# Summing the squares of two token blocks on TensorE, k-tile by k-tile, instead of on VectorE

## The chip, the cores and the metric

The kernel runs on one core of one Trainium2 chip. The metric is the device time of one execution in microseconds (us); the time before is the median of three runs. The engines are named as the profile names them: PE is TensorE (PEld its weight loads), DVE is VectorE, ACT is ScalarE, POOL is GpSimd, SP is SyncE, whose queue issues nearly all DMAs here.

## The reference, cut to what matters

One decoder layer over 2048 tokens and 1024 channels, float32. What the change touches is the first normalisation, of the layer's input x:

```
h = rmsnorm(x, g_mix) * (1.0 + sc_m) + sh_m     # x32 * rsqrt(mean(x32 * x32, over channels) + EPS) * g
proj = h @ w_in                                 # columns: q | k | v | forget gate | u
```

sc_m and sh_m come from the conditioning vector c: silu(c) @ w_ada + b_ada. After the projection come attention with a forget gate on q, k, v, a state-space scan on u (its tables are worked out in the kernel), an output projection, and a gated MLP.

## The kernel before, in words

The tokens are cut into four blocks of 512 (TB), the channels into eight k-tiles of 128 (KT). x lies transposed: a tile `xt` holds two k-tiles of one block, 128 channels on the partitions and 512 tokens along the free axis. So the sum of squares of a token runs over partitions and over k-tiles.

`load_x(b)` (L400) does this for a block. For each of the four `xt` tiles it issues a load on SP (L404), and for each of its two k-tiles ACT squares it: the first square goes straight into an accumulator `sq_acc` (L330), the seven others into a buffer `sq` of two (L333), which DVE adds to the accumulator (L334). `norm_factor` (L355) then sums over the partitions: `token_sums` (L339) takes each 128 tokens of the accumulator as weights and a column of ones as the moving operand, four matmuls into four columns of a PSUM bank `misc_ps` (L342; eight instructions in the trace). `rsqrt_mean` (L163) works out 1/sqrt on DVE in some twelve small operations on 128x4 numbers, `spread` (L362) transposes the result over all partitions on PE (L348) and ACT copies it to `rt` (L368).

`proj_u(b, ...)` (L432) uses it: `modulate` (L387) makes, for each k-tile, `h_f` = x * scale * rt on DVE (L392), stores it for blocks 2 and 3 (L395, SP), and splits it into a high half on ACT (`h_hi`, L380) and a low half on DVE (`h_lo`, L381). The projection's matmuls (L429) take three products per k-tile: high by high weight, high by low weight, low by high weight.

At the program's begin the blocks come in the order 2, 3, 1, 0. Before block 2 can be modulated, the scale and shift of the first normalisation have to be there: `ada_first` (L275) loads 32 tiles of w_ada and takes half of them through PE (L286) and half through DVE (L288, L290); each half of the channels ends with small matmuls of one moving column (L317, L299) and a small addition on DVE (`mod_gm`, `mod_sm`; L319, L294, L300). The tables of the state-space part (`ssm_tables`, L640 on, `tb_` tiles) are many small and some middling operations on DVE in the same stage, with small matmuls of their own on PE (L777, L778). Weight tiles are split into a high half on ACT and a low half on DVE as well (L77, L78).

No order is written out by hand for this stage. The code gives the operations in program order, and when the program is built, a planner lays out every engine's queue from a simulated timeline (`schedule_with_timeline_sim=True`, L1728); each engine then runs its queue in that fixed order and waits where an operand isn't ready. So an edit can change the order of instructions that it doesn't mention.

The lines of the stage:

```
rows0 = load_x(2)
wu = load_u_weights(wup, vfu_slots[4:6])
ada_first()
batches = ssm_tables(pp)
wu += load_u_weights(wup, vfu_slots[6:8])
...
for b in (2, 3, 1):
    h = proj_u(b, rows0 if b == 2 else load_x(b), wu)
```

Of the kernel before, what the change touches and what calls it, by code (L numbers as in the profile page):

```python
# [12 lines left out]
F32 = mybir.dt.float32  # L13
# [3 lines left out]
AF = mybir.ActivationFunctionType  # L17
# [5 lines left out]
P = 128  # L23
S = 2048
D = 1024
KT = D // P
NB = 4
TB = S // NB
# [11 lines left out]
XB = 6  # L40
# [3 lines left out]
HOOK = 5  # L44
EACH = 1
LEAD = 4
NSC = 2


# [62 lines left out]
def hybrid_layer(ctx, tc, x, c_t, w_ada, b_col, gains, w_flat, bf_row, a_re, a_im, log_dt,  # L112
                 sb_re, sb_im, sc_re, sc_im, dskip, glu, bglu, conv, out):
    nc = tc.nc
    V, A, G, T, Q = nc.vector, nc.scalar, nc.gpsimd, nc.tensor, nc.sync
# [20 lines left out]
    ones = const.tile([P, 1], F32, name="ones")  # L136
# [26 lines left out]
    def rsqrt_mean(ss, n, width):  # L163

        v = small.tile([P, 8], F32, name="rs_v")[:, :n]
        V.tensor_scalar(out=v, in0=ss, scalar1=1.0 / width, scalar2=EPS, op0=ALU.mult, op1=ALU.add)
        i = small.tile([P, 8], I32, name="rs_i")[:, :n]
        V.tensor_scalar(out=i, in0=v.bitcast(I32), scalar1=1, scalar2=None, op0=ALU.logical_shift_right)
        V.tensor_scalar(out=i, in0=i, scalar1=-1.0, scalar2=RSQRT_MAGIC, op0=ALU.mult, op1=ALU.add)
        y = i.bitcast(F32)  # L170
        for _ in range(3):
            t = small.tile([P, 8], F32, name="rs_t")[:, :n]
            r = small.tile([P, 8], F32, name="rs_y")[:, :n]
            V.tensor_tensor(out=t, in0=y, in1=y, op=ALU.mult)
            V.scalar_tensor_tensor(out=t, in0=t, scalar=-0.5, in1=v, op0=ALU.mult, op1=ALU.mult)
            V.scalar_tensor_tensor(out=r, in0=t, scalar=1.5, in1=y, op0=ALU.add, op1=ALU.mult)
            y = r
        return y
# [53 lines left out]
    xp = in_ctx.enter_context(tc.tile_pool(name="x", bufs=3))  # L232
# [5 lines left out]
    def misc_ps():  # L238
        return in_ps.tile([P, 512], F32, name="misc_ps", tag="misc", bufs=1)
# [85 lines left out]
    sq_pool = [xp]  # L325

    def sum_squares(acc, first, src, cols, eng, tmp=None):

        if first:
            A.activation(acc[:, cols], src, AF.Square)  # L330
        else:
            sq = sq_pool[-1].tile([P, TB], F32, name="sq", tag="sq", bufs=2)[:, cols] if tmp is None else tmp
            A.activation(sq, src, AF.Square)  # L333
            eng.tensor_tensor(out=acc[:, cols], in0=acc[:, cols], in1=sq, op=ALU.add)  # L334

    def sq_acc():
        return sq_pool[-1].tile([P, TB], F32, name="sq_acc", tag="sq_acc", bufs=2)

    def token_sums(ps, acc, s0, n):  # L339

        for i in range(n):
            T.matmul(ps[:, i : i + 1], lhsT=acc[:, (s0 + i) * P : (s0 + i + 1) * P], rhs=ones[:, 0:1],  # L342
                     start=True, stop=True)

    def over_channels(ps, r, n):

        for i in range(n):
            T.transpose(ps[:, i * P : (i + 1) * P], r[:, i : i + 1].broadcast_to([P, P]), ident)  # L348
# [6 lines left out]
    def norm_factor(acc, ps_fn, direct=False):  # L355

        ps = ps_fn()
        token_sums(ps, acc, 0, 4)
        r = rsqrt_mean(ps[:, 0:4], 4, D)
        return spread(r, ps_fn, direct)  # L360

    def spread(r, ps_fn, direct=False):  # L362
        ps = ps_fn()
        over_channels(ps, r, 4)
        if direct:
            return ps
        rt = sq_pool[-1].tile([P, TB], F32, name="rt", tag="rt", bufs=RT)
        A.copy(rt, ps)  # L368
        return rt
# [28 lines left out]


    def load_x(b):  # L400
        rows, acc = [], sq_acc()
        for j in range(4):
            xt = xp.tile([P, 2, TB], F32, name="xt", tag="xt", bufs=XB)
            Q.dma_start(xt, x[b, j])  # L404
            rows.append(xt)
            for a in range(2):
                sum_squares(acc, j == 0 and a == 0, xt[:, a], slice(0, TB), V)
        return rows, norm_factor(acc, misc_ps)

    def load_u_weights(pool, slots):  # L410
        res = []
        for so, sn, n in slots:
            hi = pool.tile([P, sn], F32R, name="wu_hi", tag="wu_hi", bufs=4)
            lo = pool.tile([P, sn], F32R, name="wu_lo", tag="wu_lo", bufs=4)
            weights.load(so, sn, hi, lo)
            res.append((hi, lo))
        return res
# [644 lines left out]
    def attention(blocks, lead=0):  # L1062

        heads = [(b, h) for b in blocks for h in range(H)]
        steps, cur = att_max(*heads[0])
        for f in steps:
            f()
        for j, (b, h) in enumerate(heads):
            nsteps, nxt = att_max(*heads[j + 1]) if j + 1 < len(heads) else ([], None)
            msteps, done = att_main(b, h, *cur), 0  # L1070
            for n, f in enumerate(msteps):
                f()
                todo = min(len(nsteps), -(-len(nsteps) * (n + 1) // max(1, len(msteps) - lead)))
                while done < todo:
                    nsteps[done]()
                    done += 1
            cur = nxt
# [31 lines left out]
    with tc.tile_pool(name="prep", bufs=1) as pp, tc.tile_pool(name="wu", bufs=1) as wup:  # L1109
# [5 lines that stand above are left out]
        marks = []  # L1115
        for b in (2, 3, 1):
            h = proj_u(b, rows0 if b == 2 else load_x(b), wu)
            marks.append(mark[0])
        batches(marks + marks[-1:])
        rows0 = load_x(0)  # L1120
        proj_qkv(1, h, pair_ps(qs_psum))
        ada_late(4, "gf")
        h = proj_u(0, rows0, wu)
        ada_late(3, "sf")
        forget()
        ada_cols()
        fold_gain(mod["gf"], 8)
        ada_late(2, "tm")
# [105 lines left out]
    def h2_of(b, xs, acc):  # L1234
        ps_fn = ff_ps if b == 0 else op_ps
        return modulate(xs, norm_factor(acc, ps_fn, True), mod["gf"], mod["sf"])
# [308 lines left out]
    with tc.high_priority():  # L1545
        x1, sq1 = out_proj(0, mt)
        yt += [y_tile(d, F32) for d in range(8)]
        h2 = h2_of(0, x1, sq1)
    attention((1, 2, 3), LEAD)
    att_ctx.close()  # L1550
# [17 lines left out]
    def block3():  # L1568

        steps = up_rows(ops["f1"], h_rows(xb, spread(ops["r3"], op_ps, True)))  # L1570
        rows = next(steps)
        for nm in ("b11", "b21"):
            ops[nm] = [split_h(f) for f in rows[nm]]
        next(steps)
        ops["t1"] = [split_h(f, parts=late_pair(late, 14)) for f in rows["t1"]]
        next(steps)
        spare = [f("hh", [P, TB + 2 * (f is vq_a)], F32R)[:, 0:TB] for f in (vq_b, vq_c, vq_a) for _ in range(2)]
        ops["t2"] = [split_h(f, parts=late_pair(late, 14) if k < 3 else spare[0:2]) for k, f in enumerate(rows["t2"])]
        next(steps)
        ops["b22"] = [split_h(rows["b22"][k], parts=spare[2 + 2 * k : 4 + 2 * k]) for k in range(2)]  # L1580
        return steps, rows

    for b in range(2):
        i = 0
        for g, n in enumerate(FFG):
# [7 lines left out]
            sq = sq_acc() if last else None  # L1593
            if last:
                mt = mix_t(b + 1)
            for d in range(8):
# [12 lines left out]
                if last and d == OPD + 1:  # L1609
                    with behind():  # L1610
                        if b == 0:
                            h2 = modulate(x1n, spread(r, op_ps, True), mod["gf"], mod["sf"])
                        else:
                            ops["r3"] = r
                            steps, rows = block3()
# [117 lines left out]
```

## Time and profile before

| | us |
|---|---|
| median of three runs | 2649.02 |
| the three runs | 2645.67, 2649.02, 2649.54 |
| the profiled execution | 2642.66 |
| its span, first to last instruction | 2641.0 |
| PE busy in the span | 2553.1 |
| DVE busy | 1925.0 |
| ACT busy | 1237.9 |

The mean granted clock of PE over the span is 0.984. A busy PE need not be PE at its peak: matmuls are pipelined, their ends are modelled, and in stages where the granted clock is below 1 the same matmul takes longer. In a timeline row stand the start, the duration, engine, line, operation, output and inputs, shape and count, and in brackets the idle time of the engine before it and what ended it. Where one row holds several instructions, its duration is that of the whole row. Instructions on DVE and ACT overlap a little, so the next one can start before the one before has ended.

### The profile page before, as it was taken

The numbers are of one execution on the slowest core, as the hardware profiler recorded it, in microseconds if no ns is written. First come the engines' busy times: TensorE is split into PE (matmuls) and PEld (weight loads), VectorE is DVE, ScalarE is ACT, GpSimd is POOL, SyncE is SP. The second block draws the span as 40 slices with busy tenths as digits, with TensorE's granted clock in tenths as the row PEclk, the third lists the DMA queues.
The fourth block names the chain that finished last, engine by engine and source line by source line (L and its number), as shares of the span: only waits on it lengthen the run. The fifth ranks groups of instructions, "written<-read, shape, count | busy, mean of one in ns | idle before, by whom it ended". The sixth has DMA issues, their size and how long they took to land. (4 is left out here: it accounts for less than half of the span.)

```text
span 2641.0 us, 35638 instructions
## 1 busy us (share of the span) xinstructions
PE 2553.1 (97%) x12343; PEld 2067.4 (78%) x12343; DVE 1925.0 (73%) x3568; ACT 1237.9 (47%) x2056; POOL 190.2 (7%) x146
## 2 busy tenths in 40 slices
PE   6999999999999999999999999999989999999997
PEld 3888877887788887888778887888758888887886
DVE  7989588966887877886877777675687777773343
ACT  3423255553564545564645555565544444442222
POOL 0001000000000000000000000000043333320000
PEclk8999999999999999999999999999989999999999
DMA  8486987667466565655657565547632332346563
GB/s 311 155 272 212 302 261 208 204 195 248 139 200 218 187 199 164 204 191 186 200 174 231 170 202 168 188 164 259 222 104 104 112 112 96 122 150 249 168 233 99
DMA packets 265925, 500.63 MB, mean 190 GB/s; under 512 B 27120, under 2 KB 111984, under 8 KB 265744
## 3 DMA queue, kind: packets, MB, share of 16 engines
q1 hardware_dynamic: 263920, 493.10, 56.7%
q0 software_dynamic: 1280, 4.20, 0.4%
q8 instruction: 98, 1.61, 0.2%
q10 hardware_dynamic: 544, 1.05, 0.1%
q14 instruction: 83, 0.68, 0.1%
HBM read 371.17 MB, written 127.01 MB: 189 GB/s over the span
## 5 line engine op out<-in xcount | busy, mean ns | idle before, releaser
L78 DVE TENSOR_TENSOR w_lo<-w_raw,w_hi 128x1024 fp32r<-128x1024 f32 (+2 forms) x219 | 235.8, 1078 | 206.9 <-ACT w_hi L77 205.0
L77 ACT CAST w_hi<-w_raw 128x1024 fp32r<-128x1024 f32 (+2 forms) x219 | 203.1, 929 | 354.2 <-DMA w_raw<-in_w_flat 110.1
L1248 PE MATMUL ff_ps<-h_lo,w_hi 128*128 128x512 f32 x704 | 279.9, 398 | 0.8 <-DVE h_lo L381 0.8
L1248 PE MATMUL ff_ps<-h_hi,w_lo 128*128 128x512 f32 x704 | 280.2, 398 | 0.0
L1248 PE MATMUL ff_ps<-h_hi,w_hi 128*128 128x512 f32 x704 | 279.4, 399 | 0.0
L999 DVE TENSOR_TENSOR pl<-pf,ph 128x512 fp32r<-128x512 f32 (+1 forms) x320 | 194.8, 618 | 19.6 <-ACT ph L998 18.4
L998 ACT CAST ph<-pf 128x512 fp32r<-128x512 f32 (+1 forms) x320 | 177.9, 569 | 60.9 <-PE o_ps L1008 54.8
L1007 DVE TENSOR_TENSOR acc<-acc,pf 128x512 f32<-128x512 f32 (+2 forms) x264 | 159.2, 604 | 28.2 <-ACT pf L997 25.7
L1248 PEld LDWEIGHTS ff_ps<-h_lo,w_hi 128*128 128x128 f32 x704 | 133.4, 190 | 29.5 <-DVE h_lo L381 1.1
L1248 PEld LDWEIGHTS ff_ps<-h_hi,w_lo 128*128 128x128 f32 x704 | 133.4, 189 | 29.3 <-DMA w_lo<-wlo 0.4
L997 ACT ACTIVATE pf<-sc_ps 128x512 f32<-128x512 f32 (+2 forms) x184 | 98.4, 539 | 123.1 <-PE sc_ps L988 73.0
L1248 PEld LDWEIGHTS ff_ps<-h_hi,w_hi 128*128 128x128 f32 x704 | 133.2, 189 | 28.8 <-issue 0.2
L107 ACT CAST w_hi<-w_raw 128x1024 fp32r<-128x1024 f32 (+2 forms) x100 | 96.4, 964 | 102.9 <-PE ff_ps L1222 41.1
L1281 PE MATMUL ff_ps<-act_lo,w_hi 128*128 128x512 f32 x352 | 139.5, 397 | 0.0
L1280 PE MATMUL ff_ps<-act_hi,w_hi 128*128 128x512 f32 x352 | 139.3, 398 | 0.2 <-ACT rt L368 0.2
L1282 PE MATMUL ff_ps<-act_hi,w_lo 128*128 128x512 f32 x352 | 139.3, 397 | 0.0
L949 DVE TENSOR_REDUCE mx<-sc_ps 128x1 f32<-128x512 f32 (+2 forms) x164 | 97.5, 599 | 49.1 <-PE sc_ps L944 24.6
L1008 PE MATMUL o_ps<-ph,vv 128*128 128x512 f32 (+1 forms) x320 | 120.5, 377 | 2.3 <-ACT ph L998 2.2
L1371 PE MATMUL up_x<-hh,w_hi 128*128 128x512 f32 x352 | 113.4, 401 | 7.6 <-DVE hh L378 5.9
L1012 PE MATMUL o_ps<-pl,vv 128*128 128x512 f32 (+2 forms) x312 | 115.9, 374 | 0.9 <-DVE pl L999 0.9
L1371 PE MATMUL up_z<-hh,w_hi 128*128 128x512 f32 x352 | 111.9, 399 | 1.4 <-ACT vz L1387 1.4
L1472 PE MATMUL acc_ps<-act,w_hi 128*128 128x512 f32 (+1 forms) x276 | 104.9, 380 | 2.2 <-ACT w_hi L77 1.5
(575 smaller groups left out, 6705.0 us busy)
## 6 DMA issues: line engine op xcount, KB each, us to landing
w_raw<-in_w_flat SPq DMA_DIRECT2D x193, 512.0 KB
w_lo<-wlo SPq DMA_DIRECT2D x68, 512.0 KB
wlo<-w_lo SPq DMA_DIRECT2D x52, 512.0 KB
w_raw<-in_w_flat SPq DMA_DIRECT2D x64, 384.0 KB
kb<-kb SPq DMA_DIRECT2D x80, 256.0 KB
vv<-v SPq DMA_DIRECT2D x80, 256.0 KB
w_raw<-in_w_flat SPq DMA_DIRECT2D x64, 320.0 KB
act<-act SPq DMA_DIRECT2D x32, 512.0 KB
```

The lines of the kernel that those rows point to most:

```text
L77: nc.scalar.copy(hi[:, :n], raw[:, :n])
L78: nc.vector.tensor_tensor(out=lo[:, :n], in0=raw[:, :n], in1=hi[:, :n].bitcast(F32), op=ALU.subtract)
L998: A.copy(ph[:, cs], pf[:, cs])
L999: V.tensor_tensor(out=pl[:, cs], in0=pf[:, cs], in1=ph[:, cs].bitcast(F32), op=ALU.subtract)
L1007: eng.tensor_tensor(out=acc[j][:, cs], in0=acc[j][:, cs], in1=pf[:, cs], op=ALU.add)
L1008: T.matmul(o_ps[:, cs], lhsT=vt[:, i, :], rhs=ph[:, cs], start=first, stop=False)
L1012: T.matmul(o_ps[:, cs], lhsT=vt[:, i, :], rhs=pl[:, cs], start=False, stop=(b > 0 and ch == b - 1 and i == 3))
L1248: T.matmul(ps, lhsT=lt, rhs=rt, start=(n == 0), stop=(n == 23))
L1280: T.matmul(ps, lhsT=a, rhs=ah[:, ts], start=(c == 0), stop=False)
L1281: T.matmul(ps, lhsT=a, rhs=al[:, ts], start=False, stop=False)
L1282: mark[0] = T.matmul(ps, lhsT=bb, rhs=ah[:, ts], start=False, stop=(c == n - 1))
L1371: mark[0] = T.matmul(ps, lhsT=lt, rhs=rt, start=(first and n == 0), stop=(n == 11), skip_group_check=not first)
```

## The change

A list `SQPE` names the blocks that take a new path, 2 and 3. For them `load_x_pe` replaces `load_x`. It loads the same tiles in the same way. All eight squares go into the buffer `sq` of two, and behind each of them PE takes it as weights, 128 tokens at a time, against the column of ones: four matmuls per k-tile that accumulate over the eight k-tiles in the four columns of one PSUM bank. So DVE's seven adds per block and the accumulator go, and the one group of four matmuls at the end of a block becomes eight groups, one per k-tile. `rsqrt_mean` and `spread` follow as before. Blocks 1 and 0 keep the old path.

```diff
@@ -44,6 +44,7 @@
 HOOK = 5
 EACH = 1
 LEAD = 4
+SQPE = (2,3,)
 NSC = 2
 
 
@@ -398,6 +399,8 @@
 
 
     def load_x(b):
+        if b in SQPE:
+            return load_x_pe(b)
         rows, acc = [], sq_acc()
         for j in range(4):
             xt = xp.tile([P, 2, TB], F32, name="xt", tag="xt", bufs=XB)
@@ -406,6 +409,22 @@
             for a in range(2):
                 sum_squares(acc, j == 0 and a == 0, xt[:, a], slice(0, TB), V)
         return rows, norm_factor(acc, misc_ps)
+
+    def load_x_pe(b):
+
+        rows, ps = [], misc_ps()
+        for j in range(4):
+            xt = xp.tile([P, 2, TB], F32, name="xt", tag="xt", bufs=XB)
+            Q.dma_start(xt, x[b, j])
+            rows.append(xt)
+            for a in range(2):
+                k = 2 * j + a
+                sq = sq_pool[-1].tile([P, TB], F32, name="sq", tag="sq", bufs=2)
+                A.activation(sq, xt[:, a], AF.Square)
+                for i in range(4):
+                    T.matmul(ps[:, i : i + 1], lhsT=sq[:, i * P : (i + 1) * P], rhs=ones[:, 0:1],
+                             start=(k == 0 and i == 0), stop=(k == KT - 1), skip_group_check=True)
+        return rows, spread(rsqrt_mean(ps[:, 0:4], 4, D), misc_ps)
 
     def load_u_weights(pool, slots):
         res = []
```

## The prediction

> **What bounds the kernel now.** I read the page's busy times first, then the busy time by stage for the first 165 us, because the two blocks that the change touches lie there, then PE's waits, and last the timelines of PE, DVE and ACT in those stages. The page:
>
> ```profile
> span 2641.0 us, 35638 instructions
> ...
> PE 2553.1 (97%) x12343; PEld 2067.4 (78%) x12343; DVE 1925.0 (73%) x3568; ACT 1237.9 (47%) x2056; POOL 190.2 (7%) x146
> ```
>
> PE is busy 97% of the span, so 88 us of PE idle time are all that there is to hide work in or to win. The stages (length, then busy us and instruction count of PE, PE's weight loads, DVE, ACT and POOL, then granted clock, DMA share, GB/s):
>
> ```profile
> 7.20:13.60 6.40, 0.00 (x0) 0.00 (x0) 4.89 (x8) 5.07 (x9) 0.00 (x0) 1.00 1.02 403
> 13.60:44.40 30.80, 28.81 (x100) 11.41 (x100) 24.34 (x92) 5.87 (x8) 0.00 (x0) 0.94 0.98 345
> 44.40:50.40 6.00, 0.03 (x1) 0.03 (x1) 6.00 (x26) 3.35 (x7) 0.00 (x0) 0.55 0.94 346
> 50.40:59.70 9.30, 6.62 (x33) 6.20 (x33) 9.30 (x29) 5.70 (x9) 0.00 (x0) 0.68 0.67 224
> 59.70:70.10 10.40, 10.36 (x48) 9.84 (x48) 9.44 (x49) 4.77 (x9) 0.00 (x0) 0.56 0.76 259
> 70.10:86.00 15.90, 12.33 (x102) 11.88 (x102) 15.90 (x65) 5.93 (x30) 0.00 (x0) 1.00 0.26 84
> 86.00:96.00 10.00, 9.96 (x44) 8.53 (x45) 8.79 (x25) 4.81 (x8) 0.00 (x0) 0.50 0.84 270
> 96.00:165.00 69.00, 67.44 (x491) 60.80 (x491) 63.47 (x226) 23.25 (x53) 1.62 (x2) 1.00 0.60 184
> ```
>
> Up to 44.40 the DMA share is 0.98 and more: the loads set the pace. From 44.40 to 59.70 DVE is busy 15.30 of 15.30 us and PE only 6.65: DVE sets the pace. From 59.70 to 70.10 both are full, PE at a granted clock of 0.56. From 86.00 on PE is busy 77.40 of 79.00 us, so whatever delays or advances PE's work at 86 is carried on. The change is therefore worth what it moves PE's arrival at 86.
>
> PE's waits up to 130 us (total, times, longest) name one wait above all in the DVE-paced stage:
>
> ```profile
> PE proj_ps L429 <- ACT h_hi L380: 11.1, 4, 6.0
> ```
>
> PE's timeline at the places that matter:
>
> ```profile
> 13.63 1.83 PE L342 MATMUL misc_ps<-ones,sq_acc 128*128 128x1 f32 x8 [13.63 <-DVE sq_acc L334]
> ...
> 41.94 1.05 PE L317 MATMUL prep_ps<-ones,ada_acc 128*128 128x1 f32 x8
> 43.33 1.02 PE L299 MATMUL prep_ps<-ones,ada_acc 1*128 1x1 f32 x8 [0.35 <-DVE ex_r L508]
> 50.37 0.59 PE L429 MATMUL proj_ps<-wu_hi,h_hi 128*128 128x264 f32 x1 [6.02 <-ACT h_hi L380]
> ...
> 62.87 1.70 PE L342 MATMUL misc_ps<-ones,sq_acc 128*128 128x1 f32 x8
> ...
> 68.95 0.28 PE L429 MATMUL proj_ps<-wu_hi,h_hi 128*128 128x264 f32 x1
> ...
> 82.25 0.60 PE L348 MATMUL misc_ps<-ident,rs_y 128*128 128x128 f32 x4
> ...
> 86.03 0.59 PE L429 MATMUL proj_ps<-wu_hi,h_hi 128*128 128x264 f32 x1 [2.86 <-ACT h_hi L380]
> ```
>
> The reader is to see the price of one group of four token sums (eight instructions in the trace): 1.83 us at 13.63 and 1.70 at 62.87, where PE is slow, and 1.05 us at 41.94 for the same form (128x128 weights, one moving column) where PE is fast. One such group per block becomes eight.
>
> **The change, part by part.** On DVE seven adds per block go. Their price, and the step that follows block 3's sums:
>
> ```profile
> 46.89 0.69 DVE L334 TENSOR_TENSOR sq_acc<-sq_acc,sq 128x512 f32<-128x512 f32 x1
> 47.49 0.17 DVE L523 CAST ex_ei<-ex_e 128x16 int32<-128x16 f32 x1
> ...
> 84.48 1.41 DVE L392 SCALAR_TENSOR_TENSOR h_f<-xt,mod_gm,rt 128x512 f32<-128x512 f32 x2
> ```
>
> An add takes 0.69 us, but the next instruction starts 0.60 us after it, so it occupies the queue for 0.60; seven are 4.2 us. For block 2 they lie in 7.20:13.60, where DVE waits for squares and the loads set the pace: worth nothing there. For block 3 they lie between 46.89 and about 60, in the stage that DVE paces: up to 4.2 us.
>
> On PE seven more groups per block come, 7 x 1.83 = 12.8 us at the slow price, 7 x 1.05 = 7.4 us at the fast one. On ACT the eight squares stay eight; no DMA is added or removed, and none moves in the program. What is new is a wait: the two square buffers are freed by PE and no longer by DVE, so a square waits for the group two before it, and what is queued on ACT behind it waits too:
>
> ```profile
> 7.11 0.61 ACT L333 ACTIVATE sq<-xt 128x512 f32<-128x512 f32 x1
> ...
> 44.53 0.63 ACT L330 ACTIVATE sq_acc<-xt 128x512 f32<-128x512 f32 x1
> ...
> 49.59 0.72 ACT L380 ACTIVATE h_hi<-h_f,mod_sm 128x512 fp32r<-128x512 f32 x1 [1.35 <-DVE h_f L392]
> 50.22 1.13 ACT L333 ACTIVATE sq<-xt 128x512 f32<-128x512 f32 x2
> 51.26 0.71 ACT L380 ACTIVATE h_hi<-h_f,mod_sm 128x512 fp32r<-128x512 f32 x1
> ...
> 56.31 0.71 ACT L380 ACTIVATE h_hi<-h_f,mod_sm 128x512 fp32r<-128x512 f32 x1
> ...
> 82.89 0.59 ACT L368 COPY rt<-misc_ps 128x512 f32<-128x512 f32 x1
> ```
>
> Block 2. The first square is there at about 7.2, so PE can begin 6.4 us before its present 13.63. Of the 12.8 us that leaves 6.4, and PE's idle time in 13.60:44.40, 30.80 - 28.81 = 2.0 us, takes up some: at worst the second half of the modulation, whose sums now start at 41.94, comes 4.4 us late. But PE sits idle for 6.0 us just behind it, so only DVE's start on the next stage counts, and DVE has 30.80 - 24.34 = 6.5 us of slack before that. I put +1.0 us on the path, between 0 and 4.4; nearer to 0 because both slacks are there in rows. Without that slack it would be the 4.4.
>
> Block 3. PE's idle time in 44.40:50.40 and 50.40:59.70 is 5.97 + 2.68 = 8.65 us. At the slow price 12.8 - 8.65 = 4.2 us don't fit and push PE's work in 59.70:70.10, which has no gap. At the fast price 7.4 fit whole, and PE is up to 4.2 us earlier with DVE's relief. So this term lies between -4.2 and +12.8 (no gap used at all). I take +4.2, since the groups' own row in this stage, at 62.87, has nearly the slow price, and the granted clock is 0.55, 0.68 and 0.56 in the three stages.
>
> [...] The rows first: PE was at work on one-column groups from 41.94 to 44.35, and the next stage's clock is 0.55; in 59.70:70.10 PE is never idle, with the group of 62.87 in its midst, and a matmul costs 0.28 us again only at 68.95. [...] The rows speak against counting such groups as busy: two groups' worth of them did not hold the clock at 44.40.
>
> Behind block 3's sums: its factor is spread over channels by PE at 82.25 (transposes queued behind block 2's last projection), copied at 82.89 to 83.48, and used by DVE at 84.48, since DVE is busy with tables until then. With DVE 4.2 us ahead, the use starts when the copy ends: 84.48 - 83.48 = 1.0 us of the 2.86 us gap before 86.03 closes: -1.0 us. It is 0 if DVE stays where it is, and -2.9 if the transposes move ahead of the projection.
>
> Sum: +1.0 + 4.2 - 1.0 = +4.2 us at 86, carried to the end. The profiled execution took 2642.66 us (its span and 1.66 around it), 6.4 below the median of 2649.02; with the change it would take 2646.9, and the median 2653.2.
>
> **The rivals.** Faster: DVE's relief comes through whole. For it: DVE is full in 44.40:59.70 and PE waits 6.02 us at 50.37. Against it: the groups need PE's slow time just there. It decides if the groups, filling PE's idle 6.0 us from 44.40, hold the clock near 1.00, so that a group costs about 1.05 us and all seven fit into the 8.65 us. It gives -4.2, and with the whole gap at 86.03 another -2.9: 2649.0 - 7.1 = 2641.9.
>
> Slower: ACT is held by its square buffers. The first group could run from 45.2; at 1.83 each the third ends at 50.7 and the fourth at 52.5. The sixth square, done at 51.35 now, then ends at 53.1, and the halves behind it (51.26) come 1.9 us late; with the projection's matmuls in between (twelve to a k-tile, at 9.96 us for the 44 instructions of 86.00:96.00, where PE is as slow, about 2.7 us) groups five and six end near 58.9, so that the half at 56.31 starts after the eighth square, at 59.5: 3.2 us late in a stage where PE waits for exactly these halves. On top of +1.0 and +4.2 that is +8.4: 2657.4. It decides if squares five to eight wait for PE by more than 1 us each. For it: all the halves are on ACT's queue among the squares. Against it: the planner may put the squares behind the halves.
>
> Nothing seen: the planner, which lays out each engine's order from a simulated timeline, gives groups and gaps to each other so that 0 remains, 2649.0. Its order may also differ far behind the stage, by an amount that no row shows; I let that widen the range by a few us on either side.
>
> **How the numbers follow.** 0.2% is 5.3 us, about what a measurement of this kernel can tell from no change. The forecast, +4.2, gets 0.40: 0.25 of it within 0.2%, 0.15 slower. The faster rival gets 0.27: 0.22 faster, 0.05 within. The slower one gets 0.23: 0.21 slower, 0.02 within. Nothing seen gets 0.10: 0.08 within, 0.02 faster. Together faster 0.24, same 0.40, slower 0.36. The range runs from 2640, just past the faster rival, to 2662, the slower rival with the rest of block 2's bound (3.4 us) on it and a little for the order; since both signs hold much of the chance, the forecast's own range is 2648 to 2658.
>
> **What would show it.** Right: 64 instructions of token sums per block (eight groups), all on PE before about 62 us, at 1.7 to 1.9 us a group; PE's first wait of 6.02 us shrunk to under 2; the 59.70:70.10 work ending some 4 us later; the first matmul of block 3's projection about 4 us after 86.03; PE busy from there on as before. Wrong: groups of about 1.05 us in block 3 and a clock near 1.00 from 45 to 60; that first matmul earlier than 86.03; or an end that moves by much more than it does, which would mean the planner changed the order behind it.

## The result

| | before | after |
|---|---|---|
| median | 2649.28 us (4 runs, 2645.67 to 2654.47) | 2663.48 us (4 runs, 2659.89 to 2665.41) |
| profiled execution | 2642.66 us | 2659.89 us |
| its span | 2641.0 us | 2658.0 us |

The ratio is 1.0052, with an interval from 1.0038 to 1.0067: the change costs 14.2 us, where 4.2 were forecast, and the median lies 1.5 us above the range. The page of the changed kernel:

```profile
span 2658.0 us, 35828 instructions
...
PE 2576.6 (97%) x12455; PEld 2090.4 (79%) x12455; DVE 1917.0 (72%) x3554; ACT 1239.0 (47%) x2056; POOL 190.3 (7%) x146
```

PE has 112 instructions and 23.5 us of busy time more, DVE 8.0 us less. The stages, with the same limits and columns as in the prediction:

```profile
13.60:44.40 30.80, 29.21 (x118) 15.22 (x117) 23.74 (x86) 9.15 (x14) 0.00 (x0) 1.00 1.00 356
44.40:50.40 6.00, 6.00 (x31) 3.26 (x31) 6.00 (x47) 2.66 (x4) 0.00 (x0) 1.00 1.04 391
50.40:59.70 9.30, 9.30 (x69) 9.27 (x68) 9.30 (x52) 6.56 (x14) 0.00 (x0) 0.85 0.77 263
59.70:70.10 10.40, 10.23 (x84) 10.02 (x83) 10.40 (x43) 6.25 (x24) 0.00 (x0) 0.97 0.59 196
70.10:86.00 15.90, 14.96 (x122) 13.20 (x121) 15.76 (x55) 3.46 (x7) 0.00 (x0) 1.00 0.50 152
86.00:96.00 10.00, 6.78 (x38) 5.91 (x37) 10.00 (x24) 5.19 (x10) 0.00 (x0) 0.83 0.65 207
```

From 44.40 to 59.70 PE is now busy 15.30 us instead of 6.65, and its granted clock is 1.00 and 0.85 instead of 0.55 and 0.68. The places of PE's timeline that answer to those shown of before:

```profile
7.35 8.66 PE L425 MATMUL misc_ps<-ones,sq 128*128 128x1 f32 x40 [7.35 <-ACT sq L423]
...
26.49 1.05 PE L425 MATMUL misc_ps<-ones,sq 128*128 128x1 f32 x8
...
44.75 0.36 PE L318 MATMUL prep_ps<-ones,ada_acc 128*128 128x1 f32 x2
...
48.96 1.05 PE L425 MATMUL misc_ps<-ones,sq 128*128 128x1 f32 x8
...
54.09 2.66 PE L425 MATMUL misc_ps<-ones,sq 128*128 128x1 f32 x22
61.13 1.62 PE L425 MATMUL misc_ps<-ones,sq 128*128 128x1 f32 x14
...
79.66 0.65 PE L349 MATMUL misc_ps<-ident,rs_y 128*128 128x128 f32 x4
...
82.52 0.40 PE L448 MATMUL proj_ps<-wu_hi,h_hi 128*128 128x264 f32 x1
```

Block 3's eight groups cost about 1 us each (eight instructions 1.05 us at 48.96, twenty-two 2.66 us at 54.09). The first matmul of its projection starts at 82.52 instead of 86.03, with no wait ahead of it. So in this trace the stage that the change touches is 3.5 us faster, and the loss is made later. The 3.5 us are rough: five traces have this work in this early order, and the matmul starts at 82.52, 83.28, 83.34, 85.96 (with one small copy more on DVE) and 86.34 in them; in three with the work and the order of before it starts at 86.03, 86.81 and 87.27. The means, 84.3 and 86.7, are 2.4 us apart.

To find where the loss is made, both traces are cut at three points at which PE has done the same instructions, token sums apart: one beside 165 us, one beside 352 us, and the point behind which PE's queue is in the same order again, at 629.68 us before and 643.42 after. Busy time by stretch, in the kernel before and in the changed one:

```profile
0.00:164.13 164.13, 134.68 (x811) 107.95 (x812) 142.20 (x515) 61.17 (x130) 4.05 (x24) 0.90 0.69 229
164.13:352.10 187.97, 179.29 (x1126) 156.21 (x1124) 145.50 (x261) 57.27 (x104) 16.09 (x24) 0.99 0.85 275
352.10:629.68 277.58, 266.93 (x1552) 219.61 (x1550) 225.90 (x457) 146.51 (x302) 1.04 (x2) 0.99 0.72 217
```

```profile
0.00:160.66 160.66, 143.65 (x924) 118.55 (x924) 139.53 (x513) 60.84 (x130) 6.04 (x26) 0.98 0.71 235
160.66:356.77 196.11, 183.32 (x1125) 160.45 (x1124) 140.20 (x252) 57.06 (x104) 13.67 (x21) 0.97 0.84 266
356.77:643.42 286.65, 273.24 (x1551) 223.99 (x1550) 226.32 (x455) 147.95 (x302) 1.04 (x2) 0.96 0.69 208
```

The first stretch is 3.5 us shorter, the second 8.1 longer, the third 9.1 longer, and what is left of the span 3.3 longer. In the second PE does the same 1124 matmuls in both kernels, with 4.0 us more of busy time (183.32 against 179.29, at a clock of 0.97 against 0.99) and 4.1 us more of idle time (12.79 against 8.68). PE's waits in it, before and after:

```profile
PE vq_ps L429 <- DVE qk_lo L468: 3.3, 2, 3.1
PE prep_ps L792 <- ACT tb_wb L793: 2.3, 2, 1.2
PE qs_ps L462 <- DVE qk_lo L468: 1.4, 1, 1.4
PE sc_ps L944 <- ACT pf L997: 1.3, 1, 1.3
```

```profile
PE qs_ps L481 <- DVE qk_lo L487: 4.0, 2, 3.8
PE vq_ps L448 <- DVE qk_lo L487: 2.5, 1, 2.5
PE vq_ps L481 <- DVE qk_lo L487: 2.3, 1, 2.3
PE prep_ps L796 <- ACT tb_wb L812: 2.1, 1, 2.1
PE prep_ps L811 <- ACT tb_wb L812: 1.9, 2, 1.4
```

No line of the change is among them. They are the q, k and v projections of blocks 1 and 0 and the tables of the state-space part. In the built programs the queues of all engines stand in another order up to the third cut (PE's differs at 2752 of its first 3124 places, token sums left out) and, two DMA issues apart, in the same order from there on.

One caution: single traces differ by several us. Behind the third cut, the fourteen traces of this study that share the order there, and whose weights and other buffers lie as far apart as before, take 2009 to 2019 us, whatever was changed early. And the traced execution can be an outlying one: that of the next experiment lies 6.2 us above its kernel's median. Verdicts therefore rest on medians and on ratios to the kernel before, which was run beside each kernel (medians of 2647.5 to 2649.9 us).

### The profile page after: what moved, and what is told of

It is laid out like the page before. It is cut to its first block, busy times and chain, and to the rows that moved or that the text cites. A ratio compares the mean times of both kernels' runs of the same rounds, so it can differ in the third digit from the quotient of the medians.

```text
span 2658.0 us, 35828 instructions
## 1 busy us (share of the span) xinstructions
PE 2576.6 (97%) x12455; PEld 2090.4 (79%) x12455; DVE 1917.0 (72%) x3554; ACT 1239.0 (47%) x2056; POOL 190.3 (7%) x146
## 3 DMA queue, kind: packets, MB, share of 16 engines
q10 hardware_dynamic: 544, 1.05, 0.1%
```

## The experiments: work or order

Two theories. "Work": PE is the bound, and its new busy time comes out at the end in any order. "Order": the new work is harmless, and the loss is made by the order that the planner chose behind the stage. They are told apart by giving one kernel's work the other's order. The kernels record the order of every engine's queue and hold the instructions to it by edges that fix the order of issue and add no wait for a result. The planner still places token sums and DVE's adds:

```diff
+def pin(nc, tc):
+    ...
+        seq = [mine[int(j)] for j in table[at : at + n]]
+        ...
+        for prev, ins in zip(seq, seq[1:]):
+            tc.add_manual_dep(ins, prev.name, mybir.DependencyInfo(mybir.DependencyClass.NoSync,
+                              mybir.DependencyReason.DATA), reason="pin")
...
         hybrid_layer(tc, *args)
+        pin(nc, tc)
```

Holding an order costs nothing by itself: the kernel before, held in its own order with 160 unused bytes added, takes 2649.03 us (ratio 0.9996, 0.9987 to 1.0004; it stands in the table of places further down).

**The new work in the order of before.** The diff above, in the changed kernel, with the table of before.

> The changed kernel's work in the order of the kernel before: edges of issue order alone hold the instructions of each engine (PE, DVE, ACT, POOL and the DMA queues) in the order that the planner gave the kernel before; only the 64 token sums of the two blocks stand where the planner puts them. Theory 'order' (the loss comes from the planner's changed order between 165 and 640 us, not from the work): between 2643 and 2651 us, no loss. Theory 'work' (PE is the bound, its extra busy time less the 6.3 us by which it begins earlier shows at the end, in any order): about 2649 + 14 = 2663, between 2658 and 2667.

2661.38 us, ratio 1.0052 (1.0039 to 1.0065). "Order" fails as it was put, "work" seems right. But the trace shows the loss in another place than the changed kernel's:

```profile
0.00:178.91 178.91, 159.36 (x923) 130.55 (x924) 132.04 (x501) 61.20 (x130) 3.85 (x23) 0.88 0.65 210
178.91:370.10 191.19, 182.22 (x1125) 158.53 (x1124) 145.91 (x262) 57.40 (x104) 16.27 (x24) 0.97 0.83 271
```

The first stretch is 14.8 us longer than before (178.91 against 164.13), the second only 3.2 (in the slowest of its six executions). Its timeline and its stage from 59.70 show where:

```profile
32.02 1.08 PE L736 MATMUL misc_ps<-ident,rs_y 128*128 128x128 f32 x4 [3.52 <-DVE rs_y L564]
...
54.56 6.99 PE L812 MATMUL misc_ps<-ones,sq 128*128 128x1 f32 x32 [0.79 <-ACT sq L810]
```

```profile
59.70:70.10 10.40, 10.40 (x49) 10.40 (x50) 5.91 (x18) 4.38 (x6) 0.00 (x0) 0.50 0.69 200
```

Block 2's transposes stand ahead of the other matmuls in that order and hold PE for 3.52 us, and block 3's groups fall into PE's slow time at 1.75 us each (thirty-two instructions in 6.99). That is the slow price of the prediction: it is what the sums cost in the order of before, which the planner did not keep.

**The old work in the new order.** The same pin in the kernel before, with the table of the changed kernel.

> The kernel before with its adds on DVE and its two groups of token sums, in the order that the planner gave the changed kernel. Theory 'order': the loss is there without any of the new work, 2658 to 2668 us. Theory 'work': 2646 to 2652, as before.

2664.10 us, ratio 1.0061 (1.0047 to 1.0074): the whole loss, with none of the new work. "Work" falls.

```profile
0.00:164.72 164.72, 128.88 (x812) 102.55 (x813) 148.36 (x529) 60.64 (x130) 6.04 (x26) 0.93 0.69 229
164.72:367.58 202.86, 186.02 (x1125) 162.46 (x1124) 140.19 (x250) 57.16 (x104) 12.58 (x21) 0.94 0.80 257
```

PE reaches the first cut 0.6 us late and loses 14.9 us in the second stretch.

**The new work, its own order up to 165 us, the order of before from there.** The pin with a table made of the two.

> The changed kernel, with its own planned order up to about 165 us (744 PE instructions beside the token sums) and the order of the kernel before from there on. Its first 165 us were 3.4 us ahead in the changed kernel's trace. Theory 'order': the 3.4 us are kept, 2645 us (2642 to 2649). Theory 'work': idle time that the sums filled early comes back later in this order too, and the end is at 2663 (2658 to 2667).

2646.24 us, ratio 0.9989 (0.9979 to 0.9998). The same work as the changed kernel's, 17.2 us faster (2663.48 - 2646.24), with nothing changed but the order behind 165 us. (A second kernel of this work and order, with all its buffers moved alike, takes 2649.49 us, 14.0 less than the changed one; it stands further down.) "Order" holds in this form: ahead of 165 us the order of before does not suit the new work, and behind 165 us the changed order is worse for either work.

```profile
0.00:161.70 161.70, 142.38 (x923) 116.82 (x924) 140.05 (x514) 61.02 (x130) 6.04 (x26) 0.99 0.70 234
161.70:352.39 190.69, 181.01 (x1126) 157.45 (x1124) 137.88 (x248) 57.24 (x104) 12.74 (x21) 0.98 0.84 270
```

**How far the loss is spread.** The same, with the changed order up to 357 us.

> As the run with the changed kernel's order up to 165 us, but its own order now reaches to about 357 us of its trace (1789 PE instructions beside the token sums), and the order of the kernel before begins only there. In the changed kernel's trace the stretch from 161 to 357 us is 196.1 us long, in the kernel before 188.0 and in the run with the graft at 165 us 190.7. If the loss of the changed order is spread over the whole stretch up to 640 us: 2646.2 + 5.4 to 8.2, so 2651 to 2655. If it lies in the stretch up to 357 us alone: 2658 or more. If it lies behind 357 us alone: 2643 to 2649.

2654.74 us, ratio 1.0025 (1.0014 to 1.0037): 8.5 us of the 17.2 are made in the second stretch, the other 8.7 behind it. It is no single wait.

**Is any new order worse?** The old work, in the orders planned for block 3 alone (`SQPE = (3,)`) and for block 2 alone (`SQPE = (2,)`):

> The kernel before, its work unchanged, in the order that the planner gives a kernel in which block 3 alone is summed on PE: a second changed order, to see whether the one of the full change is a rare bad one. If the order of the kernel before is a good one among many and any new plan of the early stage loses it: 2655 to 2668 us. If the full change met with a rare bad order: 2646 to 2653.

> The kernel before, its work unchanged, in the order that the planner gives a kernel in which block 2 alone is summed on PE: a third order for the same work. If the order of the kernel before is a good one among many: slower than 2649 by 5 us or more, as the two others tried (2656.78 and 2664.1). If those two were bad luck: 2644 to 2653.

2656.78 us, ratio 1.0039 (1.0023 to 1.0055), and 2650.12 us, ratio 1.0002 (0.9991 to 1.0013). The second missed what "a good one among many" asked for. Four planned orders of one and the same work take 2649, 2650, 2657 and 2664 us: a plan is a draw over 15 us, and not every other draw loses. What in the change made the planner choose the worst of them stays open.

## The experiments: what the new work is worth

With the order held as in the run of 2646.24 us, the two halves of the change can be taken one by one. The groups without the relief (adds kept, the groups into columns that nobody reads), the relief without the groups (seven k-tiles left out of the sum), and the old work:

```diff
 e12: V.tensor_tensor(out=acc, in0=acc, in1=sq, op=ALU.add)
+     T.matmul(ps[:, 4 + i : 5 + i], lhsT=sq[:, i * P : (i + 1) * P], rhs=ones[:, 0:1], start=True, stop=True)
 e15: A.activation(sq, xt[:, a], AF.Square)
+     if k < KT - 1:
+         continue
```

> DVE's seven adds per block kept beside PE's seven groups (into columns that nobody reads), in the order that gave 2646.24 without the adds. If the early gain (2.4 to 3.5 us at 165 us) comes from DVE's relief: it is gone, and the end is at 2649 to 2655. If it comes from PE's groups holding the granted clock up from 44 to 60 us: it is kept, 2643 to 2649.

> DVE's relief alone: for blocks 2 and 3 the adds are gone and PE has one group of token sums per block as before, over the last k-tile's squares (the other seven k-tiles are left out of the sum), in the order that gave 2646.24 with all sums on PE. If the early gain comes from DVE's relief: kept, 2642 to 2648, and at 165 us 2 us or more ahead of the kernel before. If PE's groups are what brings it, by the clock: gone, 2649 to 2653.

> The kernel before's work (adds on DVE, one group per block on PE) in the order that gave 2646.24 with the sums on PE: the changed kernel's order up to 165 us, its own from there. If DVE's relief is worth 6 us and PE's groups cost 3.5, as e3, e12 and e15 say in this order: 2649 (2646 to 2652). If that order's early stage is itself a gain or a loss: more than 3 us away from 2649.

| medians, one order | one group per block | eight groups |
|---|---|---|
| adds on DVE | 2647.89 (ratio 1.0000, 0.9987 to 1.0012) | 2652.35 (1.0011, 0.9998 to 1.0024) |
| no adds | 2642.63 (0.9973, 0.9961 to 0.9985) | 2646.24 (0.9989, 0.9979 to 0.9998) |

DVE's relief is worth 5.3 and 6.1 us, PE's groups cost 4.5 and 3.6: the change is worth -1.7 us, too little to be told from nothing. The four kernels ran on different occasions; by the ratios, which take that out, the relief is 7.2 and 5.8 us, the groups cost 2.9 and 4.2, and the change is worth -2.9. The intervals with and without the adds stand apart or just touch; those with and without the groups overlap. All three runs fell as the relief theory had them. The clock theory falls by the first of them, whose stages from 44.40 and 50.40 are:

```profile
44.40:50.40 6.00, 5.36 (x28) 2.69 (x27) 6.00 (x41) 0.00 (x0) 0.00 (x0) 1.00 0.69 268
50.40:59.70 9.30, 8.21 (x60) 7.01 (x60) 9.30 (x40) 5.38 (x8) 0.00 (x0) 0.99 0.47 169
```

PE's clock is 1.00 and 0.99, and nothing is won: DVE, busy 15.30 of 15.30 us, still sets the pace. Nor are the groups what holds the clock in the first of the two stages. The old work in this order, with one group per block, has

```profile
44.40:50.40 6.00, 5.89 (x24) 2.47 (x23) 6.00 (x47) 1.77 (x3) 0.00 (x0) 1.00 0.91 359
50.40:59.70 9.30, 3.75 (x27) 3.52 (x28) 9.30 (x49) 4.94 (x9) 0.00 (x0) 0.80 0.60 210
```

The order itself puts matmuls of the modulation there. Only in the second stage do the clocks differ, 0.99 with the groups and 0.80 without them, and from 59.70 to 70.10 it is the other way, 0.68 and 0.85.

**Block 3 alone** (`SQPE = (3,)`, its own order to 165 us, that of before from there):

> Block 3 alone summed on PE, block 2 on DVE as before, in the order planned for it up to about 165 us and in the order of the kernel before from there. If block 2's sums bring nothing, since the loads set the pace there, and block 3's adds were what DVE lacked time for: 2643 to 2649, as with both blocks. If block 2's groups, which keep PE at work from 7.4 us on, are what keeps the granted clock near 1.00 in the stages from 44.40 to 59.70, the early gain is lost: 2648 to 2656.

2646.79 us, ratio 0.9995 (0.9986 to 1.0004), at a clock of 0.56 and 0.55 in the two stages just shown. By the medians block 2's sums bring nothing, as the prediction had it. The trace alone would not say so: its PE reaches the first cut at 168.01, 6.3 us behind the run with both blocks, but its execution is 2.7 us above the median of its kernel and the other's 2.9 below; the two early orders differ as well.

**Adds and sums together in the order of before** (the first edit above, with the table of before):

> The kernel before in its own order, with PE's new work beside DVE's old work: for blocks 2 and 3 every square from the second on goes through DVE's add and also through a group of four token sums on PE, into four columns that nobody reads. It computes the same, with 14 groups more on PE and no add less on DVE. Theory 'order': 2649 to 2654, at most the sums' own place in the early stage. Theory 'work': the extra PE time in full and no relief, 2663 to 2668. If e1 is fast and this is slow, the adds taken off DVE pay for PE's sums.

2656.72 us, ratio 1.0036 (1.0023 to 1.005), between the two expectations and 7.8 us above the kernel before. In its trace PE is 7.5 us late at the first cut (171.60) and 8.9 at the third (638.58), which a single trace can't tell from 7.5: in that order the groups cost some 7.5 us before 165 us even where no result waits for them (their square buffers do). And in that order taking the adds off as well brings nothing: 2661.38 us without them, 2656.72 with them. The relief of 5 to 7 us belongs to the other order.

## The experiments: fp32r squares, and a gain that was not theirs

**Squares and ones in fp32r**, two equal columns in place of one, in an order made as above:

```diff
-                sq = sq_pool[-1].tile([P, TB], F32, name="sq", tag="sq", bufs=2)
+                sq = sq_pool[-1].tile([P, TB], F32R, name="sq_r", tag="sq", bufs=2)
...
-                    T.matmul(ps[:, i : i + 1], lhsT=sq[:, i * P : (i + 1) * P], rhs=ones[:, 0:1],
+                    T.matmul(ps[:, 2 * i : 2 * i + 2], lhsT=sq[:, i * P : (i + 1) * P], rhs=ones_r,
```

> Both blocks on PE, with the squares and the column of ones stored as fp32r, so that a token sum is one pass over two equal columns in place of an f32 product of one column (the squares are rounded); its own planned order up to 165 us, the order of the kernel before from there. If PE's time for the sums is hidden in the early stage already (DVE and the loads set the pace there): 2642 to 2649, no different from the f32 sums in the same order. If PE's time for the sums counts there, most of it is saved, and the end comes at 2634 to 2642.

> The kernel of the earlier run with fp32r squares (2631.47 us) once more, nothing changed. If its 18 us belong to the kernel: 2629 to 2635, with matmuls from 700 to 1300 us again 1% closer together. If they belonged to that occasion: 2649 to 2656, since behind 165 us that run was 5 us late before its matmuls gained.

2631.47 us, ratio 0.9936 (0.9923 to 0.9949), and again 2630.89, ratio 0.9927 (0.9913 to 0.9941). In the first one's trace a group is four matmul instructions, 64 for both blocks, where the f32 groups of the changed kernel are eight, 128 for both. It looked like the second theory, but at 400 us that trace is 7 us behind before, and it gains only behind 660 us, in matmuls that the edit doesn't touch. The edit had also put two small tiles into SBUF, which moved the weights' buffers by 32 bytes per partition and most others by 160. Four kernels take squares and places apart (e10 fp32r with nothing moved, e9 and e11 everything moved alike, e16 f32 with every buffer where it lay in the fp32r runs):

```diff
 e10:
+    ones_4 = const.tile([P, 4], F32R, name="ones")
+    ones, ones_r = ones_4[:, 0:1].bitcast(F32), ones_4[:, 2:4]
 e9, e11:
+    pad = const.tile([P, 40], F32, name="pad")
+    V.memset(pad, 0.0)
 e16:
+    pad = const.tile([P, 2], F32, name="pad")
+    V.memset(pad, 0.0)
...
+        ss = small.tile([P, 4], F32, name="ss4", tag="ss4")
+        V.tensor_copy(ss, ps[:, 0:4])
```

> The fp32r squares once more, in the same order as in the run with them, with the columns of ones in the padding of the tile that holds them, so that no buffer of the later stages moves. If the buffers' place made the gain: 2648 to 2656 us (the run was 7 us behind at 400 us). If the fp32r squares made it: 2629 to 2635.

> The kernel before, its work and its order unchanged, with a tile of 160 bytes per partition that nobody reads put behind the column of ones (one memset on DVE), so that every later buffer in SBUF lies 160 bytes further up, as in the run with fp32r squares. That run was 7 us behind the kernel before at 400 us and 8.5 us ahead at 2550 us, in the same order: its matmuls from 700 to 1300 us start 214.3 ns apart on average, those of the kernel before 215.8. If the buffers' place makes that difference: 2629 to 2638 us. If it came from the fp32r squares: 2646 to 2652, as before.

> Both blocks on PE in f32, the changed kernel's order up to 165 us and the order of the kernel before from there (which gave 2646.24), with the 160 bytes put in. If the buffers' place is worth 16 us whatever the early stage does: 2627 to 2634. If not: 2643 to 2649.

> Both blocks on PE in f32 in the order that gave 2646.24, with the two small tiles of the fp32r run added (8 bytes beside the ones, four small tiles behind the norm's), so that every buffer lies where it lay in that run. If the buffers' places gave its 18 us: 2627 to 2634. If not: 2643 to 2651.

| | moved: weights, the rest | us | ratio |
|---|---|---|---|
| fp32r squares | 0, 0 | 2653.43 | 1.0014 (1.0004 to 1.0024) |
| before | 160, 160 bytes | 2649.03 | 0.9996 (0.9987 to 1.0004) |
| both blocks in f32, order of the graft | 160, 160 | 2649.49 | 0.9999 (0.9989 to 1.0009) |
| both blocks in f32, order of the graft | 32, 160 | 2627.95 | 0.9909 (0.989 to 0.9928) |

It is neither the squares nor the move; what is left is the distance between the weights and the buffers behind them, which is 128 bytes more in the first two fp32r runs and in the last row, and as before in the others. The last kernel is that distance alone, in the kernel before:

```diff
     mark = [None]
+    gap = small.tile([P, 8], F32, name="gap", tag="gap")
+    V.memset(gap, 0.0)
```

> The kernel before in its own order and with its own work, with four small tiles of 32 bytes that nobody reads put between the weights' buffers and those of the moving operands (one memset), so that the second lie 128 bytes further up and the weights stay where they are. If the distance between weights and moving operands makes the 18 to 20 us of the runs with 32 and 160 bytes: 2627 to 2635. If something else in those kernels does: 2645 to 2653.

2632.29 us, ratio 0.9939 (0.9919 to 0.9958): four unused tiles of 32 bytes are worth 15 us. The kernel with both blocks on PE, the grafted order and this distance (2627.95) is the fastest of all, ahead of both kernels, and most of its lead has nothing to do with the change.

The fp32r squares themselves brought nothing: with the buffers in place they are 4 us slower than before, in an order with a seam of its own at 165 us.

## Why the prediction was wrong

**The bound of the stage** was read rightly. DVE's adds were on the path from 44.40 to 59.70, and seven of them at 0.60 us were costed at 4.2 us of relief; measured, in one held order, 5.3 and 6.1 by the medians, 7.2 and 5.8 by the ratios.

**Block 2**, +1.0 us. The second half's small matmuls start at 44.75 instead of 41.94, within its bounds, and at the end nothing of it is seen: block 3 alone takes as long as both.

**Block 3**, +4.2 us. Wrong in the price of a group, and so in the sign. The slow 1.83 us was taken from rows of the old order (1.83 us at 13.63, 1.70 at 62.87), where PE waits 6.02 us before 50.37 and the clock is 0.55, 0.68 and 0.56 in the three stages from 44.40 on. The planner put the groups between other matmuls, and they cost about 1 us at a clock of 1.00, 0.85 and 0.97. Block 3's transposes, which follow its last group, come at 79.66 instead of 82.25: blocks 2 and 3 together make -2.6 us in this trace, not +5.2. All three signs of error that the prediction named came: the fast groups, the earlier matmul, the end that moves by much more than it. In the order of before the slow price was right: 1.75 us a group, and 14.8 us late at the cut.

The prediction's reading of the rows, that such groups by themselves did not hold the clock, agrees with two later traces. In the run with block 3 alone twenty-four of these instructions stand behind one another and take 1.76 us a group, in a stage at 0.56:

```profile
47.00 5.28 PE L812 MATMUL misc_ps<-ones,sq 128*128 128x1 f32 x24 [2.80 <-ACT sq L810]
```

In the changed kernel PE has one-column matmuls alone from 52.90 to 56.75, and a matmul of 264 columns takes 0.29 us at 56.81 and 0.42 from 57.09 on. What the prediction missed is that the new order puts other matmuls into the gap: the modulation's (L287 in the changed kernel) run at 45.04, 46.52 and 48.01, where the last of them started at 41.41 before. With them PE is busy 6.00 of 6.00 us from 44.40 to 50.40, at a clock of 1.00, where it was busy 0.03 us at 0.55 before. That a busy PE is enough is not shown: from 59.70 to 70.10 it is busy 10.36 of 10.40 us before, at 0.56. And the run with adds and groups shows that the higher clock, 1.00 and 0.99, won nothing while DVE set the pace: 2652.35 us, against 2647.89 for the old work in the same order.

**The gap before 86.03**, -1.0 us, was right, and for the reason given: the copy of block 3's factor now ends at 80.93, and DVE's use of it starts at 80.96.

```profile
80.34 0.59 ACT L369 COPY rt<-misc_ps 128x512 f32<-128x512 f32 x1 [2.16 <-PE misc_ps L349]
80.96 1.41 DVE L393 SCALAR_TENSOR_TENSOR h_f<-xt,mod_gm,rt 128x512 f32<-128x512 f32 x2
```

From the transposes to the matmul it is 2.86 us instead of 3.78, 0.9 us less; PE's wait is gone because matmuls of the tables now stand in it. At that matmul the sum in this trace is therefore -3.5 us and not +4.2.

**"+4.2 us at 86, carried to the end"** is the step that failed. That PE is busy 77.40 of 79.00 us from 86 on says that a shift is carried if the queues behind it stay as they are, and they did not. With the order of before kept behind 165 us nothing of this loss is seen: 2.4 us ahead at that matmul by the means, 2.7 and 0.4 at the end (2646.24 against 2648.92, and 2649.49 against 2649.86 with all buffers moved alike), which is too little to say how much of a shift is carried. In the planner's own order the 3.5 us that were ahead became 14.2 behind. The prediction named a changed order, but as a few us on either side of the range; it measured 17.2 us, or 14.0 by the second kernel.

**The slower rival** gave a time nearer to the measured one, for a wrong reason. ACT did wait for its square buffers, five times for 9.5 us in all up to 165 us. But only two of these waits are block 3's, 1.50 us at its third square and 2.42 at its sixth, where the rival needed more than 1 us at each from the fifth to the eighth, and PE still came to 82.52 ahead of time:

```profile
ACT sq L423 <- PE misc_ps L425: 9.5, 5, 3.0
```

**The faster rival** had the sign right up to 165 us and half the size: -7.1 at that matmul, where the trace has -3.5. Its condition, groups that hold the clock, is not what the runs show: 0.56 in the stage with twenty-four of the instructions in a row. **Nothing seen**, the planner giving groups and gaps to each other so that 0 remains, is near to what the work alone is worth, -1.7 us; the planner's order behind the stage was the cost.

## What to carry to other kernels

Where a planner lays out the queues, an edit early in the program is two edits, its work and a new order for everything behind it, and the second can be the larger by far: here some 2 us won and 14 to 17 lost. Hold the order fixed before judging the work, and compare where PE reaches the same instruction in both traces, not what the change touched. Take more than one trace for it: the same work in the same order came to one matmul at 82.52 and at 86.34. Before a few tenths of a per cent are put down to an edit that allocates anything, ask what else it moved in SBUF.

## What was not expected of the hardware

The place of buffers in SBUF changed the pace of matmuls that nothing else touched: the kernel with the gap takes 2632.29 us, the kernel before beside it 2647.47. In the built kernel before, `w_hi` starts at byte 28224 of a partition and `h_hi` at 59072. With `h_hi` at 59200 and all buffers behind the weights moved as well (those laid out from the other end of SBUF stay, attention's among them), the matmuls of the feed-forward part are some half a per cent shorter. The costliest groups of PE before, then with everything moved by 160 bytes, then with the gap of 128 (busy us, mean ns of one):

```profile
L1248 PE MATMUL ff_ps<-h_hi,w_lo 128*128 128x512 f32 x704 | 280.2, 398 | 0.0
L1281 PE MATMUL ff_ps<-act_lo,w_hi 128*128 128x512 f32 x352 | 139.5, 397 | 0.0
```

```profile
L1653 PE MATMUL ff_ps<-h_hi,w_lo 128*128 128x512 f32 x704 | 280.2, 398 | 0.0
L1686 PE MATMUL ff_ps<-act_lo,w_hi 128*128 128x512 f32 x352 | 139.5, 397 | 0.0
```

```profile
L1653 PE MATMUL ff_ps<-h_hi,w_lo 128*128 128x512 f32 x704 | 278.9, 396 | 0.0
L1686 PE MATMUL ff_ps<-act_lo,w_hi 128*128 128x512 f32 x352 | 138.8, 395 | 0.0
```

The modelled ends hide a part of it. By their starts, the matmuls between 700 and 1300 us that follow each other within 215 to 300 ns lie 232.8 ns apart before, 232.6 with everything moved, 231.1 with the gap and 230.3 in the three runs with weights moved by 32 bytes and the rest by 160, at a granted clock of 1.00 in all of them. Behind the third cut these four runs take 1989 to 1994 us, the fourteen others with that order 2009 to 2019. What the rule is, and which buffers it is about, was not tried; that 230.3 and 231.1 stand at the same 128 bytes more says that this distance is not all of it.
